# Block sums of the first MLP matrix: formed by transfers into DRAM instead of by VectorE

## The chip, the cores and the metric

The kernel runs on one core of one Trainium2 chip. The metric is device time in microseconds (us), the median over repeated executions of the same program. A profile is one further execution, taken with the hardware profiler; its times count from the first instruction.

## The reference, cut to what matters

One inference step of one layer. 576 token rows (512 of a prompt, 64 of eight short samples) are normalised and go through two parallel branches, RWKV-7 time mixing and differential attention, which sigmoid gates merge. Then comes the MLP, which the change touches:

```python
m = gate_a * (o_a @ lp['w_br_a']) + gate_b * (o_b @ lp['w_br_b'])
x = x + m @ lp['w_out']
hn = rmsnorm(x, lp['g_ffn'], NORM_EPS)
x = x + jnp.square(jax.nn.relu(hn @ lp['w_up'])) @ lp['w_down']
```

`w_up` is 1024 x 4096 and `w_down` 4096 x 1024, all in 32-bit floats.

## The kernel before, in words

Data lie transposed: channels on the 128 partitions, the 576 tokens along the free axis, mostly in two halves of 288. A 32-bit product is made from three matmuls: each weight tile is split into a rounded half `hi` (ScalarE, `act`) and a rest `lo` (VectorE, `tt`), and so are the activations.

The order of work is: the q, k and v products of the four attention heads with the attention itself between them (`qkv(h)`, `prompt`, `sample`), the RWKV pairs (`rwkv(hp)`, `chain(pr)`) with the products for `z` and the gates as filling for TensorE, the branch products (`branch_b`, then `ps_bra`), `w_out` (`ps_wo`), and the MLP (`up_pair`, `down`).

A scheduler writes the order of every engine's queue at build time. It takes instructions by priority as they become ready. `prio(at)` sets a priority; instructions outside of it have the running number of the program. Loads of weights (`load`, line 150) stand under `FEED`, ahead of all others, and wait for one of three `raw` slots; matmuls stand under `FILL`, behind all others. `tc.issue_after(ins)` ties instructions behind a given one; the loads of lines 416 to 422 and the cache pages (line 614) are tied behind the first q, k and v loads in that way. Once written, each queue runs strictly in its order on the chip. SyncE (SP) issues nearly all loads; GpSimd (POOL) issues the stores of `kTo`, `vTo`, `ob_d`, `Ss` and `Sp`, and also computes `pow` for the norms (`rpow`, lines 243 and 760).

The product with `w_up` is a Strassen-Winograd scheme on 2 x 2 blocks. For each of 16 pairs of row tiles `f1`, `f2 = f1 + 1`, the two halves along the contraction give `a11`, `a12` (of `f1`) and `a21`, `a22` (of `f2`). `up_pair` loads both rows (tile `a`, 512 KB each, line 1188), and VectorE forms four sums of blocks in tiles `s12` and `s34` (shown as `s` in the profile):

```python
tt(s12[:, 0], a21, a22, ADD)
tt(s12[:, 1], s12[:, 0], a11, SUB)
...
tt(s34[:, 0], a11, a21, SUB)
tt(s34[:, 1], a12, s12[:, 1], SUB)
```

`halve` then splits `s12`, the first row, `s34` and `a22`; seven products of 12 matmuls each follow (line 1224: `ua`, `ub`, `uc`, `ud`, `ux`), and VectorE and ScalarE combine and square the results. From the fourth pair on, four `down` products of 24 matmuls (`ps_dn`) follow each pair.

Of the kernel before, what the change touches and what calls it, by code (L numbers as in the profile page):

```python
# [8 lines left out]
F32 = mybir.dt.float32  # L9
F32R = mybir.dt.float32r  # L10
I32 = mybir.dt.int32
AF = mybir.ActivationFunctionType
# [3 lines left out]
P = 128  # L16
# [9 lines left out]
DFF = 4096  # L26
# [15 lines left out]
def tile_hybrid_step(ctx, tc, xT, xsT, ktab, vtab, s0T, ptab, w_in, vecs, w2a2, g2, lamv,  # L42
                     w_bra, w_brb, w_out, w_up, w_down, cst, bias_p, bias_s,
                     yT, kTo, vTo, Sp, Ss, sh):
    nc = tc.nc
# [9 lines left out]
    ring = {"job": 0}  # L55

    def act(out, in_, func=AF.Copy, **kw):
        ring["act"] = AE.activation(out=out, in_=in_, func=func, **kw)  # L58

    def tt(out, a, b, op, eng=None):  # L60
        ins = (eng or VE).tensor_tensor(out=out, in0=a, in1=b, op=op)  # L61
        if eng is None:
            ring["tt"] = ins

    def stt(out, a, s, b, op0, op1):
        VE.scalar_tensor_tensor(out=out, in0=a, scalar=s, in1=b, op0=op0, op1=op1)
# [16 lines left out]
    FEED, LATE, FILL = -1000000, 500000, 1000000  # L83

    @contextmanager
    def prio(at):
        was, tc.cur_priority = tc.cur_priority, at
        yield
        tc.cur_priority = was

    MUL, ADD, SUB, MAX = ALU.mult, ALU.add, ALU.subtract, ALU.max
# [20 lines left out]
    c = const.tile([P, C_END], F32, name="cst_sb")  # L112
# [103 lines left out]
    def take(n):  # L216

        while waiting and n:
            if next(waiting[0], None) is None:
                waiting.pop(0)  # L220
            else:
                n -= 1
# [40 lines left out]
    oa_d = tc.dram_tile([HB, P, NT], F32, name="oa_d")  # L263
    ob_d = tc.dram_tile([HB, P, NT], F32, name="ob_d")
    gt_d = tc.dram_tile([2 * KT, P, NT], F32, name="gt_d")

    zp = pool("zp", stack=ph1)
    zw = pool("zw", 2, stack=ph1)
# [353 lines left out]
    def sample(b):  # L622
        kps = early.pop(b, None) or pages(b, True)
        if b + 1 < NB:
            early[b + 1] = pages(b + 1, True)
        vps = pages(b, False)
        pss = cbank(b % 2, f"psb{b}")
        quads = [(h, slice(32 * h, 32 * h + 32)) for h in range(HB)]

        for h, o in quads:  # L630
            mm(pss[o, P:2 * P], qbd[:, b, h], kps[1][:, h])
        with tc.issue_after(ring["mm"].ins):
            for h, o in quads:
                mm(pss[o, 0:P], qbd[:, b, h], kps[0][:, h])
            for h, o in quads:
                mm(pss[o, 256:320], qbd[:, b, h], kT[:, h, NPR:])
        sc = scs[b % 2]
        stt(sc[:, :256], pss[:, :256], 0.125, bs[:, :256], MUL, ADD)
        stt(sc[:, 256:320], pss[:, 256:320], 0.125, bs[:, 256 + 64 * b:320 + 64 * b], MUL, ADD)
        nmx = stat.tile([P, 1], F32, tag="nms", name=f"nms{b}")  # L640
        VE.tensor_reduce(out=nmx, in_=sc[:, :320], axis=AX.X, op=MAX, negate=True)
        z = stat.tile([P, 1], F32, tag="zs", name=f"zs{b}")
        act(sc[:, :320], sc[:, :320], AF.Exp, bias=nmx, accum_out=z)
        rz = stat.tile([P, 1], F32, tag="rzs", name=f"rzs{b}")
        VE.reciprocal(out=rz, in_=z)
        tt(rz, rz, cw, MUL)
        yield 1
        pt = bank(f"pts{b}")
        for j in range(3):
            tr(pt[:, j * P:(j + 1) * P], sc[:, j * P:(j + 1) * P], ident)  # L650
        pT = ap.tile([P, 3, P], F32, tag="pT", name=f"pT{b}", bufs=2)
        act(pT, pt[:, :384].rearrange("p (j r) -> p j r", j=3))
        yield 1
        po = bank(f"pos{b}")
        for j in range(3):
            for h, o in quads:
                mm(po[o, :P], pT[:, j, o], vps[j][:, h] if j < 2 else vtok[:, 4, h],
                   start=(j == 0), stop=(j == 2))
        orw = ap.tile([P, P], F32, tag="orw", name=f"orw{b}", bufs=2)
        act(orw, po[:, :P], scale=rz)  # L660
        yield 1
        pq = bank(f"pq{b}")
        mm(pq[:, :32], orw, c[:, C_SEL:C_SEL + 32])
        act(osT[:, b], pq[:, :32].rearrange("p (h q) -> p h q", h=HB))
    for h in range(HB):
        if h:
            qkv(h)
        for cc in range(2):
            GE.tensor_copy(
                out=qbd[64 * cc:64 * cc + 64, :, h, 8 * cc:8 * cc + 8],  # L670
                in_=qT[64 * cc:64 * cc + 64, h, NPR:].rearrange("p (b q) -> p b q", b=NB))
        ot = ap.tile([P, 4, P], F32, tag="ot", name=f"ot{h}", bufs=2)
        ss = stat.tile([P, 4], F32, tag="ss", name=f"ss{h}")
        qk = stacks(h)
        if h < HB - 1:
            for qb in range(4):
                feed(prompt(h, qb, ot, ss, *qk))
    waiting += [shifted(12), shifted(13)] + zs(0)
    for n in range(4):
        for unit in (prompt(HB - 1, n, ot, ss, *qk), sample(2 * n), sample(2 * n + 1)):  # L680
            feed(unit)
            fill(18)
# [366 lines left out]
    def run(*stages):  # L1049
        for hp in stages:  # L1050
            while Pt[8 + hp] is None:
                take(2)
            next(gens[hp], None)
# [2 lines left out]
    ga = [gate(g) for g in range(KT)]  # L1056
    waiting += ga[:5]
    run(0, 0)
    take(221)
    run(0, 1, 1)  # L1060
    take(106)
    run(1)
    chain(0)
    run(2, 0, 1)
    take(190)
    run(2, 3)
# [61 lines left out]
    for i, d in enumerate((0, 4, 1, 5, 2, 6, 3, 7)):  # L1128
        xr = wt_.tile([P, NT], F32, tag="xr", name=f"xr{d}")
        with prio(FEED + 1000 * (ring["job"] + 1) - 1):  # L1130
            nc.sync.dma_start(out=xr, in_=xT[:, d])
        hf = hfs[d] = wt_.tile([P, NT], F32, tag="hf", name=f"hf{d}", bufs=3)
        k = d % 4

        def ev(ps, t0, n, d=d, k=k, xr=xr, hf=hf):
            x, h = ya[:, d, t0:t0 + n], hf[:, t0:t0 + n]
            tt(x, ps, xr[:, t0:t0 + n], ADD)
            act(h, x, scale=v(V_GF + d))
            if d < 4:
                if t0 == 0:  # L1140
                    put("b11", k, h)
                else:
                    t1 = wt_.tile([P, 288], F32, tag="t", name=f"t1_{k}", bufs=4)
                    tt(t1, h, hf[:, :288], SUB)
                    hfs["t1", k] = t1
                    put("t1", k, t1)
            elif t0:
                for n, x, y in (("t2", h, hfs["t1", k]), ("t3", h, hfs[k][:, 288:])):
                    t = hfs[n] = wt_.tile([P, 288], F32, tag="t", name=f"{n}_{k}", bufs=4)
                    tt(t, x, y, SUB)  # L1150
                    put(n, k, t)
                put("b22", k, h)
            else:
                put("b21", k, h)
                t4 = wt_.tile([P, 288], F32, tag="t", name=f"t4_{k}", bufs=4)
                tt(t4, h, hfs["t2"], SUB)
                put("t4", k, t4)
        dense(w_out[d], KT, mh, ml, HALF[::1 if d < 4 else -1], ev, f"wo{d}")

        for j, (t0, n) in enumerate(HALF):  # L1160
            o = acc[:, t0:t0 + n]
            if i == 0:
                act(o, ya[:, d, t0:t0 + n], AF.Square)
            else:
                sq = cbank(j, f"sq{d}{j}")[:, :n]
                act(sq, ya[:, d, t0:t0 + n], AF.Square)
                tt(o, o, sq, ADD)
# [12 lines left out]
    def up_pair(f1):  # L1180
# [2 lines left out]
        for f in (f1, f2):  # L1183
            qs[f] = hq_pool.tile([P, 2, NT], F32R, tag="q", name=f"q{f}")
        with prio(FEED + 1000 * (ring["job"] + 1)):
            rows = [sp_.tile([P, 2, 4, P], F32, tag="raw", name=f"a{f}", bufs=3) for f in (f1, f2)]
            for r, f in zip(rows, (f1, f2)):
                nc.sync.dma_start(out=r.rearrange("p i k w -> p (i k) w"), in_=w_up[f])
        (a11, a12), (a21, a22) = ([r[:, i] for i in range(2)] for r in rows)
        s12, s34 = (sp_.tile([P, 2, 4, P], F32, tag="s", name=f"s{i}_{f1}", bufs=2) for i in (12, 34))  # L1190

        def halve(x, two, after):

# [6 lines left out]
                tt(lo, x, f32(hi), SUB)  # L1200
            return [(hi[:, i], lo[:, i]) for i in range(2)] if two else (hi, lo)

        with prio(FEED + 1000 * (ring["job"] + 1) + 90):
            tt(s12[:, 0], a21, a22, ADD)
            tt(s12[:, 1], s12[:, 0], a11, SUB)
        S1, S2 = halve(s12, True, 1)
        A11, A12 = halve(rows[0], True, 2)
        with prio(FEED + 1000 * (ring["job"] + 3) + 90):
            tt(s34[:, 0], a11, a21, SUB)
            tt(s34[:, 1], a12, s12[:, 1], SUB)  # L1210
        S3, S4 = halve(s34, True, 5)
        A22 = halve(a22, False, 7)

# [16 lines left out]
        def out(f, half, c, r=None):  # L1230

            sp = slice(288 * half, 288 * half + 288)
            r = c if r is None else r
            act(r, c, AF.Relu)
            act(r, r, AF.Square)
            act(qs[f][:, 0, sp], r)
            tt(qs[f][:, 1, sp], r, f32(qs[f][:, 0, sp]), SUB)
# [267 lines left out]
```

## Time and profile before

| what | value |
|---|---|
| median of 3 runs | 999.91 us (999.71 to 1001.37) |
| span of the profiled execution | 1004.0 us, 24422 instructions |
| TensorE matmul busy | 975.5 us (97%) |
| VectorE busy | 689.5 us (69%) |
| ScalarE busy | 497.3 us (50%) |
| GpSimd busy | 88.3 us (9%) |
| DMA | 105.75 MB, mean 105 GB/s |

The profiled execution has no time of its own beside its span, which runs from the first to the last instruction; that span is 4.1 us above the median. In the rows of the profile, PE is TensorE, PEld its weight loads, DVE is VectorE, ACT ScalarE, POOL GpSimd, SPq and POOLq the instruction queues of SyncE and GpSimd. The last two figures before a bar are the busy time of a group and the mean of one instruction in ns.

### The profile page before, as it was taken

The page shows a single profiled execution, that of the slowest core. Times are in us where ns is not written, and L with a number is a line of the kernel's source. Part 1 is how long each engine was busy: PE and PEld are TensorE (multiplying, and loading weights), DVE is VectorE, ACT ScalarE, POOL GpSimd, SP SyncE. Part 2 cuts the span into 40 slices and gives each one's busy share as a digit, 9 for nine tenths or more (in the row PEclk, how much of TensorE's full clock was granted, in tenths as well). Part 3 has the DMA queues.
Part 4 walks back from the last instruction along what each step waited for, and adds up shares of the span by engine and source line. Part 5 has one row for each costly group of instructions (what it writes and reads, how often), then busy time and mean ns, then how long its engine had stood idle before and what let it go on. Part 6 is the DMA issues. An engine that isn't in the chain of part 4 may idle for free.

```text
span 1004.0 us, 24422 instructions
## 1 busy us (share of the span) xinstructions
PE 975.5 (97%) x10012; PEld 919.9 (92%) x10012; DVE 689.5 (69%) x1459; ACT 497.3 (50%) x1094; POOL 88.3 (9%) x171
## 2 busy tenths in 40 slices
PE   8999999899999999999999999999999999999996
PEld 8999998898887878888889999999999999999996
DVE  6698666774946669445588798966666666666744
ACT  6576555354435344443344666644444444444732
POOL 2511001301010340000300000000000000000001
PEclk9999999999989989999999999999999999999998
DMA  7312673121111225222377642222222222221402
GB/s 265 142 66 88 204 221 120 54 64 45 43 47 57 69 87 171 80 70 102 106 215 237 195 152 74 95 85 95 85 85 95 84 85 85 85 84 44 128 10 95
DMA packets 50833, 105.75 MB, mean 105 GB/s; under 512 B 6066, under 2 KB 8114, under 8 KB 50594
## 3 DMA queue, kind: packets, MB, share of 16 engines
q1 hardware_dynamic: 47442, 96.95, 30.2%
q0 software_dynamic: 1648, 5.35, 1.4%
q8 instruction: 79, 1.29, 0.5%
q10 hardware_dynamic: 1632, 1.89, 0.5%
q14 instruction: 32, 0.26, 0.1%
HBM read 89.38 MB, written 14.78 MB: 104 GB/s over the span
## 4 chain that ended last, share of the span: by engine, by line
PE 86%; DVE 6%; ACT 3%; DMA 2%; issue 2%; POOL 1%; SPq 0%; DVEq 0%; POOLq 0%; ACTq 0%
PE ps_dn L72 21%; PE ps_g L72 9%; PE ps_z L72 8%; PE ua L1224 5%; PE ux L1224 5%; PE ps_wo L72 4%; PE uc L1224 3%; PE ud L1224 3%; PE ub L1224 3%; PE ps_k L72 2%; PE ps_brb L72 2%; PE pch L72 2%; PE ps_q L72 2%; PE ps_v L72 2%; PE pA L72 2%
## 5 line engine op out<-in xcount | busy, mean ns | idle before, releaser
L72 PE MATMUL ps_dn<-q,hi_dn 128*128 128x288 f32 x768 | 154.7, 296 | 0.0
L72 PEld LDWEIGHTS ps_dn<-q,hi_dn 128*128 128x128 f32 x768 | 122.8, 188 | 1.5
L72 PE MATMUL ps_dn<-q,lo_dn 128*128 128x288 f32 x384 | 113.2, 295 | 0.0
L72 PE MATMUL ps_g<-xl,hi_g 128*128 128x288 f32 x256 | 80.2, 313 | 0.0
L72 PE MATMUL ps_g<-xh,lo_g 128*128 128x288 f32 x256 | 79.3, 310 | 0.0
L72 PE MATMUL ps_g<-xh,hi_g 128*128 128x288 f32 x256 | 79.2, 310 | 0.0
L72 PEld LDWEIGHTS ps_dn<-q,lo_dn 128*128 128x128 f32 x384 | 72.1, 188 | 0.0
L72 PE MATMUL ps_z<-xh,lo_z 128*128 128x288 f32 (+1 forms) x224 | 69.6, 311 | 0.0
L72 PE MATMUL ps_z<-xh,hi_z 128*128 128x288 f32 (+1 forms) x224 | 68.3, 305 | 0.0
L72 PE MATMUL ps_z<-xl,hi_z 128*128 128x288 f32 (+1 forms) x224 | 67.6, 302 | 0.0
L61 DVE TENSOR_TENSOR ya<-ya,ps_dn 128x288 f32<-128x288 f32 x96 | 43.4, 453 | 29.3 <-PE ps_dn L72 29.3
L58 ACT ACTIVATE hi_dn<-raw_dn 128x512 fp32r<-128x512 f32 x48 | 30.1, 628 | 57.0 <-PE ps_dn L72 57.0
L1224 PE MATMUL ua<-h_b,hi 128*128 128x288 f32 x256 | 53.2, 298 | 0.0
L1224 PE MATMUL ux<-h_t,hi 128*128 128x288 f32 x256 | 52.3, 296 | 0.0
L58 ACT ACTIVATE c<-c 128x288 f32<-128x288 f32 x112 | 48.4, 439 | 7.5 <-DVE c L61 5.8
L72 PEld LDWEIGHTS ps_g<-xh,hi_g 128*128 128x128 f32 x256 | 49.0, 191 | 2.9 <-issue 1.6
L72 PEld LDWEIGHTS ps_g<-xl,hi_g 128*128 128x128 f32 x256 | 49.0, 191 | 1.9
L72 PEld LDWEIGHTS ps_g<-xh,lo_g 128*128 128x128 f32 x256 | 49.1, 192 | 1.4
L58 ACT ACTIVATE hi<-a 128x1024 fp32r<-128x1024 f32 (+1 forms) x32 | 27.1, 846 | 42.0 <-PE ps_dn L72 34.3
L72 PE MATMUL ps_dn<-q,w 128*128 128x320 f32 (+1 forms) x336 | 46.4, 298 | 0.0
L61 DVE TENSOR_TENSOR lo<-s,hi 128x1024 fp32r<-128x1024 f32 x32 | 39.2, 1225 | 10.2 <-ACT hi L58 10.0
L72 PEld LDWEIGHTS ps_dn<-q,w 128*128 128x128 f32 x336 | 45.3, 190 | 0.1
(395 smaller groups left out, 2801.7 us busy)
## 6 DMA issues: line engine op xcount, KB each, us to landing
a<-in_w_up_dram SPq DMA_DIRECT2D x32, 512.0 KB, 3.3
raw_dn<-in_w_down_dram SPq DMA_DIRECT2D x64, 256.0 KB, 2.9
raw_g<-in_w_in_dram SPq DMA_DIRECT2D x32, 256.0 KB, 3.2
raw_z<-in_w_in_dram SPq DMA_DIRECT2D x28, 256.0 KB, 3.0
gt_d<-gg SPq DMA_DIRECT2D x16, 288.0 KB, 2.5
g<-gt_d SPq DMA_DIRECT2D x16, 288.0 KB, 3.7
kp<-in_ktab_dram SPq DMA_DIRECT2D x16, 256.0 KB, 4.0
vp<-in_vtab_dram SPq DMA_DIRECT2D x16, 256.0 KB, 3.7
```

Of the source, the lines that this page charges most:

```text
L58: ring["act"] = AE.activation(out=out, in_=in_, func=func, **kw)
L61: ins = (eng or VE).tensor_tensor(out=out, in0=a, in1=b, op=op)
L72: ring["mm"] = PE.matmul(out=out, lhsT=lhsT, rhs=rhs, start=start, stop=stop)
L1224: ring["mm"] = PE.matmul(out=ps[:, :288], lhsT=l[:, k], rhs=hb[blk][:, h, k], start=start and i == 0, stop=i == 11, skip_group_check=skip)
```

## The change

The four sums are no longer made by VectorE. A scratch `us_d` of 16 x 128 x 4 x 512 floats (16 MB) in DRAM takes their place. The generator `block_sums(4)` fills it in four parts of 4 MB: for each part four copies from `w_up` into the slots 0 to 3 (1 MB each, from SP), and later four accumulating transfers (1 MB each, from POOL) that add `a22` to slot 0, `a21` to slot 2, slot 0 to slot 1 and slot 1 to slot 3. Each call of `next` writes one tick into the program: three before the heads 1 to 3, two among the samples, one before `take(221)` and one after `chain(0)`. In the seven ticks, part `t` is copied in tick `t`; its first two additions are written in tick `t + 1`, the others in `t + 2` and `t + 3`. No priority and no `issue_after` stands around them. As transfers only add, the second row of each pair enters with its sign turned; the tiles `t1` to `t4` and a scale of -1 before the Relu of `f2` turn it back.

`up_pair` now loads `s12`, row `f1` (`a1`), `s34` (512 KB each) and `a22` alone (256 KB). The first three share five `raw` slots of 4 KB per partition (before: three for `a`, two for `s`); `a22` takes one of the three `raw` slots of the ring that the `w_down` loads also use.

```diff
+    us_d = tc.dram_tile([DFF // 256, P, 4, 4 * P], F32, name="us_d")
+
+    def block_sums(n):
+
+        blk = w_up.rearrange("(g o) p (i k) w -> o i p g (k w)", o=2, i=2)
+        dst = us_d.rearrange("g p s c -> s p g c")
+        a11, a12, a21, a22 = (blk[o, i] for o in range(2) for i in range(2))
+        for t in range(16 // n + 3):
+            part = lambda a, t: a[:, n * t:n * t + n]
+            for s, src in ((0, a21), (2, a11), (1, a11), (3, a12)):
+                if t < 16 // n:
+                    nc.sync.dma_start(out=part(dst[s], t), in_=part(src, t))
+            for s, src, late in ((0, a22, 1), (2, a21, 1), (1, dst[0], 2), (3, dst[1], 3)):
+                if 0 <= t - late < 16 // n:
+                    nc.gpsimd.dma_start(out=part(dst[s], t - late), in_=part(src, t - late), accum_op=ADD)
+            yield
...
+    sums_ = block_sums(4)
     for h in range(HB):
         if h:
+            next(sums_)
             qkv(h)
...
     for n in range(4):
+        if n % 2:
+            next(sums_)
         for unit in (prompt(HB - 1, n, ot, ss, *qk), sample(2 * n), sample(2 * n + 1)):
...
     run(0, 0)
+    next(sums_)
     take(221)
...
     chain(0)
+    next(sums_)
     run(2, 0, 1)
...
-                    tt(t1, h, hf[:, :288], SUB)
+                    tt(t1, hf[:, :288], h, SUB)
...
+                    if n == "t2":
+                        stt(t, h, -1.0, hfs["t1", k], MUL, SUB)
+                    else:
+                        tt(t, h, hfs[k][:, 288:], SUB)
...
-                tt(t4, h, hfs["t2"], SUB)
+                stt(t4, hfs["t2"], -1.0, h, MUL, SUB)
...
-            rows = [sp_.tile([P, 2, 4, P], F32, tag="raw", name=f"a{f}", bufs=3) for f in (f1, f2)]
-            for r, f in zip(rows, (f1, f2)):
-                nc.sync.dma_start(out=r.rearrange("p i k w -> p (i k) w"), in_=w_up[f])
-        (a11, a12), (a21, a22) = ([r[:, i] for i in range(2)] for r in rows)
-        s12, s34 = (sp_.tile([P, 2, 4, P], F32, tag="s", name=f"s{i}_{f1}", bufs=2) for i in (12, 34))
+            s12, a1, s34 = (sp_.tile([P, 2, 4, P], F32, tag="raw", name=f"{n}{f1}", bufs=5)
+                            for n in ("s12", "a1", "s34"))
+            a22 = ring["pool"].tile([P, 4, P], F32, tag="raw", name=f"a22{f1}", bufs=3)
+            flat = lambda t: t.rearrange("p i k w -> p (i k w)")
+            nc.sync.dma_start(out=flat(s12), in_=us_d[f1 // 2, :, 0:2].rearrange("p s c -> p (s c)"))
+            nc.sync.dma_start(out=a1.rearrange("p i k w -> p (i k) w"), in_=w_up[f1])
+            nc.sync.dma_start(out=flat(s34), in_=us_d[f1 // 2, :, 2:4].rearrange("p s c -> p (s c)"))
+            nc.sync.dma_start(out=a22, in_=w_up[f2][:, 4:8])
...
-        with prio(FEED + 1000 * (ring["job"] + 1) + 90):
-            tt(s12[:, 0], a21, a22, ADD)
-            tt(s12[:, 1], s12[:, 0], a11, SUB)
         S1, S2 = halve(s12, True, 1)
-        A11, A12 = halve(rows[0], True, 2)
-        with prio(FEED + 1000 * (ring["job"] + 3) + 90):
-            tt(s34[:, 0], a11, a21, SUB)
-            tt(s34[:, 1], a12, s12[:, 1], SUB)
+        A11, A12 = halve(a1, True, 2)
...
-            act(r, c, AF.Relu)
+            act(r, c, AF.Relu, scale=-1.0 if f == f2 else 1.0)
```

More of the change, by code (lines that the diff above doesn't have):

```diff
@@ L1147, in ev @@
             elif t0:
-                for n, x, y in (("t2", h, hfs["t1", k]), ("t3", h, hfs[k][:, 288:])):
+                for n in ("t2", "t3"):
                     t = hfs[n] = wt_.tile([P, 288], F32, tag="t", name=f"{n}_{k}", bufs=4)
-                    tt(t, x, y, SUB)
+                    if n == "t2":
+                        stt(t, h, -1.0, hfs["t1", k], MUL, SUB)
+                    else:
+                        tt(t, h, hfs[k][:, 288:], SUB)
                     put(n, k, t)
```

## The prediction, made before the changed kernel ran

> **What bounds the kernel now.** I read the page first (busy shares, slices, DMA queues), then the stretches around the MLP, then the chain of waits, and last the order of the queues at the start.
>
> ```profile
> PE 975.5 (97%) x10012; PEld 919.9 (92%) x10012; DVE 689.5 (69%) x1459; ACT 497.3 (50%) x1094; POOL 88.3 (9%) x171
> DMA  7312673121111225222377642222222222221402
> q1 hardware_dynamic: 47442, 96.95, 30.2%
> PE 86%; DVE 6%; ACT 3%; DMA 2%; issue 2%; POOL 1%; SPq 0%; DVEq 0%; POOLq 0%; ACTq 0%
> ```
>
> TensorE is busy 97% of the span and is 86% of the chain that ends last; VectorE is 6% of it. The stretches (us, then busy time of PE, PEld, DVE, ACT, POOL, clock, DMA share, GB/s) say where TensorE still has idle time:
>
> ```profile
> 500.00:524.00 24.00, 22.58 (x145) 18.96 (x144) 18.79 (x36) 10.26 (x26) 3.97 (x4) 1.00 0.66 206
> 524.00:552.00 28.00, 26.60 (x196) 25.79 (x195) 22.90 (x55) 11.25 (x24) 0.00 (x0) 1.00 0.73 236
> 552.00:568.00 16.00, 15.21 (x111) 14.52 (x110) 10.68 (x24) 8.70 (x20) 0.00 (x0) 1.00 0.62 205
> 604.00:640.00 36.00, 36.00 (x267) 35.06 (x267) 31.62 (x60) 23.85 (x56) 0.00 (x0) 1.00 0.23 74
> 760.00:920.00 160.00, 160.00 (x1197) 159.07 (x1196) 108.64 (x196) 74.69 (x139) 0.00 (x0) 1.00 0.26 86
> ```
>
> From 604 us on, where the sums are used, TensorE never stops: 36.00 of 36 and 160.00 of 160. VectorE is at 88% in the first (31.62 / 36) and 68% in the second (108.64 / 160), off the path in both. The idle time ahead of the MLP is 1.42 + 1.40 + 0.79 = 3.6 us (500 to 568).
>
> **The change part by part.** *Removed: the sums.*
>
> ```profile
> L61 DVE TENSOR_TENSOR s<-a 128x512 f32<-128x512 f32 x16 | 11.0, 688 | 0.3 <-DMA a<-in_w_up_dram 0.3
> L61 DVE TENSOR_TENSOR s<-s,a 128x512 f32<-128x512 f32 x16 | 10.9, 684 | 0.0
> L61 DVE TENSOR_TENSOR s<-a,s 128x512 f32<-128x512 f32 x16 | 10.9, 684 | 0.0
> L61 DVE TENSOR_TENSOR s<-a,a 128x512 f32<-128x512 f32 x16 | 10.9, 683 | 0.0
> 555.58 7.19 DMA a<-in_w_up_dram
> 563.85 0.64 DVE s L61 x2
> ```
>
> 64 instructions, 11.0 + 3 x 10.9 = 43.7 us of VectorE. The last two rows are the chain of waits. The sums touch it at one place only, the first pair, where VectorE stands at the head of its queue for the first `a` (7.19 us) and then makes sums (0.64 us). What TensorE loses there is at most the 0.79 us of the stretch 552 to 568, so the sums are worth 0 to 0.8 us; I take -0.4. The other 15 pairs are worth nothing, since TensorE is their cover. The turned signs cost nothing: the same number of operations on the same shapes.
>
> *Added in the MLP.* Per pair 1.75 MB instead of 1 MB, four issues on SP instead of two. The DMA share there is 0.23 to 0.26; three quarters more of half the traffic leaves it under 0.4, so 15 pairs hide it. For the first pair and what is prefetched behind it, five slots of 512 KB and one of 256 KB are loaded where three of 512 KB were: 1.25 MB, 3.9 us of all engines by the 3.1 us per MB below, in a stretch at 0.62. That costs 0 to 3.9; I take 1, as ScalarE now waits for `s12` where VectorE waited for `a`. The first `s12` itself waits for the sums only if these are later than 555 us. `a22` takes one of three slots from the `w_down` loads.
>
> ```profile
> ACT hi_dn L58 <- PE ps_dn L72: 57.0, 23, 2.6
> ACT w L58 <- DMA raw_dn<-in_w_down_dram: 5.3, 8, 1.2
> raw_dn<-in_w_down_dram SPq DMA_DIRECT2D x64, 256.0 KB, 2.9
> ```
>
> The halving of `w_down` waits for matmuls to free a slot (57.0 us) and hardly for data (5.3); the rows are from the list of waits and the DMA issues. With five loads per pair in three slots, a load is still some two products (2 x 3.2 us: 24 matmuls of 12.89 / 96 each, by the chain below) ahead of its use, against 2.9 us to land: 0. Were that lead gone, each of 48 products could lose up to 2.9 us, 139 us in all, which is the upper end of this term and unlikely.
>
> ```profile
> 785.78 12.89 PE ps_dn L72 x96
> 809.87 12.89 PE ps_dn L72 x96
> ```
>
> *Added ahead of the MLP: the copies.* 16 copies of 1.05 MB (4 x 128 rows of 2 KB) on SP's queue. Queue 1 moved 96.95 MB in 30.2% of the 1004 us of its 16 engines: 0.302 x 1004 / 96.95 = 3.13 us per MB, so 3.3 us per copy if a byte that is read and written costs what a loaded one does (lower end), 6.6 us if reading and writing are charged apart (upper end). Nothing in the trace copies DRAM to DRAM; loads and stores are equally near, so I take the middle, 4.9 us, which makes 16 x 4.9 = 78 us. [...]
>
> Over the 440 us from the heads to the MLP the engines are four fifths idle, so volume is no trouble. What decides is *where in SP's queue the copies come*. They need no data and no slot, and they carry neither a priority nor a tie. What the scheduler does with such instructions, the timeline of POOL shows beside a row of the chain:
>
> ```profile
> 14.31 0.10 POOL L426 MEMSET Z<- 128x1 f32 x1 [2.59 <-DVE lo_k L61]
> 14.92 0.10 POOL L426 MEMSET Z<- 128x1 f32 x1 [0.50 <-DVE lo_v L61]
> 125.71 0.11 POOL L426 MEMSET Z<- 128x1 f32 x1 [6.01 <-DVE P L66]
> 112.78 2.27 PE ps_z L72 x17
> ```
>
> The first `Z` clearings stand in the program behind all four heads (`shifted(12)`, `shifted(13)`); their products start at 112.78 us. They run at 14.31 and 14.92, as soon as their slots are free, some 100 us ahead; the third waits for a slot until 125.71. So the place of a call of `next` sets only the rank among ready instructions. SP's queue at that time, then ScalarE's timeline, the waits of SP's queue and two rows of the DMA issues (size, us to landing):
>
> ```profile
> 10.80 1.01 SPq L150 DMA_DIRECT2D raw_q<-in_w_in_dram  x2
> 12.78 0.57 SPq L420 DMA_DIRECT2D wl<-in_w2a_dram  x1
> 14.18 0.43 SPq L422 DMA_DIRECT2D wg<-in_g_dram  x1
> 19.74 0.33 SPq L150 DMA_DIRECT2D raw_k<-in_w_in_dram  x1
> 34.33 0.33 SPq L150 DMA_DIRECT2D raw_q<-in_w_in_dram  x1
> 32.95 0.62 ACT L58 ACTIVATE hi_k<-raw_k 128x512 fp32r<-128x512 f32 x1
> 44.67 0.63 ACT L58 ACTIVATE hi_q<-raw_q 128x512 fp32r<-128x512 f32 x1 [0.34 <-ACT sc L58]
> SPq L291 <- DMA vec<-in_vecs_dram: 0.7, 1, 0.7
> bs<-in_bias_s_dram SPq DMA_DIRECT2D x1, 384.0 KB, 7.5
> raw_k<-in_w_in_dram SPq DMA_DIRECT2D x8, 256.0 KB, 3.3
> ```
>
> `wg` ends at 14.6; from there to 19.74 SP only waits for a slot, and later loads wait again until 34.33. Into the first gap the scheduler can put all copies of all four ticks, or at least some ten (0.43 to 0.57 us per issue), the rest into the second. Weight loads behind them wait twice over. Transfers of one queue share its engines in turn (`bs`, 384 KB, issued right behind the 1 MB of `bp`, takes 7.5 us, where 256 KB take 3.3), and SP stops at a limit of outstanding transfers (an `x` load, which needs nothing, waits for the transfer of `vec`).
>
> The lead of the loads is small. The second half of `raw_k` of head 1 is issued at 19.74, lands at 23.0 and is needed at 32.95: 9.9 us. `raw_q` of head 2 is issued at 34.33 and needed at 44.67. With all 16 copies ahead of it, it lands at 14.6 + 16 x 4.9 + 3.3 = 96.3, which is 51.6 us late; with 3.3 us per copy 26 us, with 6.6 us 79 us. What is late next is TensorE's `ps_q` of head 2, and nothing covers it: its queue is in order and nearly full there. Later loads come at their old distance. So the copies cost 51.6 us.
>
> *The additions.* 16 of 1.05 MB on POOL's queue, a kind that the trace does not show. Bounds: 3.3 us each, if the sum is free, to 9.9 us, if both reads and the write are charged: 53 to 158 us of engine time, mostly behind the copies. Their issue, and two `pow` steps of POOL's queue:
>
> ```profile
> L711 POOL DMA_DIRECT2D ob_d<-obs x1 | 0.8, 797 | 1.3 <-DVE nr L69 1.3
> 28.32 1.17 POOL L243 TENSOR_TENSOR r<-r,mhalf 128x5 f32<-128x5 f32 x1 [12.15 <-DVE m L1291]
> 63.99 1.04 POOL L243 TENSOR_TENSOR rr<-rr,mhalf 128x4 f32<-128x4 f32 x1 [7.72 <-DVE rr L69]
> ```
>
> 512 rows took 0.80 us to issue (`obs`), so 16 take 13 us of an engine that is 9% busy: 0. Beside weight loads they can at worst double the 3.3 us of a load, still inside the lead of 9.9: 0. [...] What they hold up is POOL: an addition waits for its copies, and behind it in the queue stand `r` (28.32, the norm that every evacuation of head 0 needs) and `rr` (63.99). The first copies land about 14.6 + 4 x 4.9 + 2 = 36, later than `r`, so I put `r` ahead and take 0; if the scheduler's order has additions ahead of `r`, the cost is below.
>
> *The sum:* -0.4 + 1 + 0 + 51.6 + 0 = +52 us. The span of the profile (1004.0) is 4.1 us above the median of 999.91; the differences apply to either, so 999.9 + 52 = 1052. I give 1050.
>
> **The rivals.**
>
> *Hidden.* If transfers to one scratch are ordered one behind the other, or if the ticks do spread them, at most two copies stand ahead of a load: 2 x 4.9 = 9.8 us against a lead of 9.9. Then all is hidden and the time is 1000, within 2. For it: the DMA share of 0.1 to 0.3 over the heads and RWKV. Against: the `Z` rows.
>
> *Partly hidden.* The copies come in four bursts of 4, one per tick. Each exposes up to 4 x 4.9 - 9.9 = 9.7 us, less what a later slot gives back: 5 to 40 us, 1005 to 1040.
>
> *POOL becomes the wait.* Additions stand ahead of `r`, and `r` comes after the last copies, at 14.6 + 78 = 93 instead of 28.3: +65, and if chained additions stand ahead of it too, two more waits of 5 to 12 us each and more: 1065 to 1100.
>
> *Faster.* VectorE's relief lets the branch products and `w_out` run closer: the 3.6 us of idle time between 500 and 568 is all there is, and it has to give over 2 us with the copies wholly hidden. Two thirds of it and a luckier order in the RWKV part: 997.5. It decides from the point where no weight load is over 9.9 us late.
>
> **How the numbers follow.** Copies ahead of the loads: 0.46 (own range 1026 to 1080). POOL: 0.11. Partly hidden: 0.16. Hidden: 0.14. Faster: 0.13. Under 0.2%, or 2 us, a measurement of this kernel can tell nothing from no change; the three runs differ by 1.7 us. So faster 0.13, same 0.14, slower 0.73. The range is 998 to 1085: it leaves out most of "faster" and the upper half of POOL's, 0.18 together.
>
> **What would show it.** In the changed profile: SP's issues of the copies (`us_d` from `w_up`) between 14 and 35 us; `raw_k`, `raw_v` and `raw_q` loads with tens of us to landing there; `hi_q` of head 2 near 95 us instead of 44.67; the slices of PE under 9 in the third to fifth fortieth and DMA at 7 or more; from 600 us on, shifted, the same 809.87 - 785.78 = 24.1 us per pair with VectorE some 2.7 us per pair less busy. The prediction is wrong if the copies lie apart over 100 us or more, if they run well under 3.3 us each, or if `w_down` halvings wait for data in the MLP.

## The result, and the profile after

The changed kernel takes 1076.1 us (1075.66 to 1079.16) against 1000.0 us (999.71 to 1001.37) of the kernel before on the same chip: 1.0768 times as long, interval 1.075 to 1.0787. The forecast was 1050 us, with a range of 998 to 1085. The profiled execution has a span of 1077.3 us, 73.3 more than that of before. One execution of a kernel below, that with plain copies, took 1177.88 us at a granted clock of 0.745 (0.976 and more in the others) and does not enter its ratio.

From the page of the changed kernel: busy shares, the slices of TensorE and of the DMA engines, the two queues, and the chain:

```profile
PE 982.9 (91%) x10012; PEld 927.2 (86%) x10012; DVE 654.9 (61%) x1395; ACT 497.6 (46%) x1094; POOL 107.0 (10%) x187
PE   8970864898999999999999999999999999999996
DMA  8999999742111111342225875343334343332312
q1 hardware_dynamic: 60498, 126.31, 36.0%
q0 software_dynamic: 10096, 22.13, 10.0%
PE 74%; DMA 9%; DVE 6%; issue 6%; ACT 3%; POOL 2%; SPq 0%; DVEq 0%; POOLq 0%; ACTq 0%
```

VectorE lost its 64 instructions (1459 to 1395), and TensorE, with the same 10012 matmuls, is no longer busy 97% of the span but 91%. The loss is at one place: the third to eighth of the 40 slices of PE read 7, 0, 8, 6, 4 and 8 where DMA stands at 9 from the second to the seventh. In the chain of waits that ended last, DMA rises from 2% to 9% of the span. Stretches of the changed kernel (columns as in the prediction):

```profile
60.00:80.00 20.00, 14.61 (x97) 14.33 (x98) 11.49 (x29) 8.83 (x28) 4.36 (x4) 0.83 1.08 302
80.00:100.00 20.00, 0.79 (x6) 0.55 (x5) 0.00 (x0) 0.00 (x0) 1.26 (x1) 0.57 1.09 270
20.00:200.00 180.00, 113.26 (x788) 107.28 (x787) 77.83 (x189) 62.16 (x166) 43.78 (x74) 0.80 1.01 261
833.00:993.00 160.00, 160.00 (x1198) 159.09 (x1197) 93.47 (x168) 74.76 (x140) 0.00 (x0) 1.00 0.37 116
```

The same 180 us of the kernel before hold 174.73 us of matmuls at a DMA share of 0.41:

```profile
20.00:200.00 180.00, 174.73 (x1558) 163.66 (x1557) 130.45 (x320) 97.72 (x252) 38.25 (x84) 0.99 0.41 130
178.43 2.18 POOL L760 TENSOR_TENSOR nr<-nr,mhalf 128x10 f32<-128x10 f32 x1
```

The second row is the first norm of the RWKV part in POOL's timeline. After the change it stands at 254.84, 76.4 us later; the whole loss of 73.3 us is made ahead of it. In the MLP's 160 us TensorE is saturated as before, while VectorE went from 108.64 to 93.47: nothing waited for it. POOL's timeline of the changed kernel, then two rows of its chain, then waits:

```profile
88.10 1.26 POOL L280 DMA_DIRECT2D us_d<-us_d  x1 [17.61 <-DMA us_d<-in_w_up_dram]
105.23 1.24 POOL L280 DMA_DIRECT2D us_d<-us_d  x1 [15.87 <-DMA us_d<-us_d]
106.00 1.55 POOL L243 TENSOR_TENSOR rr<-rr,mhalf 128x4 f32<-128x4 f32 x1
254.84 2.17 POOL L780 TENSOR_TENSOR nr<-nr,mhalf 128x10 f32<-128x10 f32 x1
```

```profile
88.10 16.84 DMA us_d<-us_d
106.46 1.09 POOL rr L243
```

```profile
POOL us_d L280 <- DMA us_d<-in_w_up_dram: 61.1, 6, 18.8
POOL us_d L280 <- DMA us_d<-us_d: 56.0, 4, 16.3
DVE ot L69 <- POOL rr L243: 48.3, 4, 30.7
```

`rr` of head 0 ran at 63.99 before; now it stands behind eight additions of POOL's queue, six of which wait there for another transfer to the scratch, the last two for 17.61 and 15.87 us; the chain runs through the last addition but one and `rr`. So three explanations were open: SP (the copies' place in SP's queue, the prediction's), POOL (its in-order queue), and volume (the engine time of all the transfers).

### The profile page after: what moved, and what is told of

Read it like the earlier page. It is cut to its first block, busy times and chain, and to the rows that moved or that the text cites. A ratio compares the mean times of both kernels' runs of the same rounds, so it can differ in the third digit from the quotient of the medians.

```text
span 1077.3 us, 24511 instructions
## 1 busy us (share of the span) xinstructions
PE 982.9 (91%) x10012; PEld 927.2 (86%) x10012; DVE 654.9 (61%) x1395; ACT 497.6 (46%) x1094; POOL 107.0 (10%) x187
## 3 DMA queue, kind: packets, MB, share of 16 engines
q0 software_dynamic: 10096, 22.13, 10.0%
## 4 chain that ended last, share of the span: by engine, by line
PE 74%; DMA 9%; DVE 6%; issue 6%; ACT 3%; POOL 2%; SPq 0%; DVEq 0%; POOLq 0%; ACTq 0%
PE ps_dn L72 19%; PE ps_g L72 9%; PE ps_z L72 7%; PE ua L1246 5%; PE ux L1246 4%; DMA us_d<-in_w_up_dram 4%; PE ps_wo L72 3%; PE uc L1246 2%; PE ub L1246 2%; PE ud L1246 2%; PE ps_brb L72 2%; PE pch L72 2%; PE ps_k L72 2%; DMA us_d<-us_d 2%; PE pA L72 2%
```

## The experiments

A ratio is to the runs of the kernel before in the same comparison (medians 1001.4 to 1002.4 us). Additional engine time is the share of queues 1 and 0 times the span, less the same of the run that has only the MLP's side.

**The copies without the additions.** The additions (the three lines that end in `accum_op=ADD`) are left out, so the scratch holds unsummed blocks; the copies stay where they are.

> The 16 additions are left out (the sums in the scratch are incomplete); the 16 copies stand at the same places of SP's queue as in the changed kernel. Theory POOL (the additions hold GpSimd's queue while they wait, and the pow steps and stores behind them come late): without additions nearly all of the +76 is gone, 1000 to 1008 us, and rr of head 0 runs near 64 us as before. Theory SP (the prediction's step: copies stand ahead of weight loads): the copies are unchanged, so at least 40 of the 76 us stay, 1040 to 1076 us, with hi_q of head 2 tens of us later than its 44.67. Theory volume (the 16 engines are full, whoever asks): half to two thirds of the bytes stay, 1020 to 1040.

Measured: 1001.91 us, ratio 0.9998 (0.9982 to 1.0015). Two stretches, the queues, and a row of SP's timeline of this run:

```profile
40.00:60.00 20.00, 19.50 (x137) 17.78 (x135) 18.49 (x48) 13.46 (x39) 6.49 (x23) 1.00 1.01 344
60.00:80.00 20.00, 19.69 (x142) 18.64 (x142) 18.14 (x45) 13.62 (x37) 3.29 (x5) 1.00 0.98 334
```

```profile
q1 hardware_dynamic: 60498, 126.31, 39.1%
q0 software_dynamic: 1648, 5.35, 1.4%
```

```profile
56.34 4.09 SPq L277 DMA_DIRECT2D us_d<-in_w_up_dram  x4
```

The engines are full (1.01, 0.98), the copies stand between the weight loads in SP's queue, and TensorE loses nothing. The prediction's main step falls: of the three forecasts only POOL's (1000 to 1008) holds. As the additions take both their waits on POOL and their engine time with them, this run does not tell these two apart.

**The MLP's side alone.** No transfers to the scratch; `up_pair` loads tiles of the same sizes from `w_up`, other blocks than the sums.

> No copies and no additions; the MLP loads tiles of the same sizes from w_up where the sums would be (the MLP's products use the second row in place of the sums). All theories that put the loss ahead of the MLP: within 0.2% of before, 998 to 1002 us; the prediction's own terms for this side were -0.4 and +1 us. If a22 in the ring of w_down or the larger loads cost anything, it shows here as over 1002.

Measured: 1002.36 us, ratio 0.9999 (0.9985 to 1.0013): within 1.4 us either way, the missing sums and the additional 0.75 MB per pair are together worth nothing (the kernel before takes 1002.42 us in the same comparison).

```profile
q1 hardware_dynamic: 52050, 109.53, 33.8%
q0 software_dynamic: 1648, 5.35, 1.5%
```

These rows give the base of the engine time: 35.3% of 998.8 = 352.6 us, and with the rows above 3.3 us per copy: (0.391 x 999.3 - 0.338 x 998.8) / 16.

**The front alone.** The kernel before with the generator and its seven ticks; the MLP does not read the scratch.

> The kernel before, with the 16 copies and 16 additions put where the change puts them; the MLP is that of before and does not read the scratch. If the whole loss is made ahead of the RWKV part, as the stretches of the changed kernel say (its first RWKV norm comes 76.4 us late, its end 73.3 us), this takes 1073 to 1079 us. If the MLP's four loads per pair have any share, it lies below: 1060 to 1070.

Measured: 1076.76 us, ratio 1.076 (1.0737 to 1.0783). That is inside the forecast of 1073 to 1079: the transfers to the scratch make the whole loss.

**POOL freed.** Copies and additions in the same order, but what stands behind the additions leaves POOL's queue (a reciprocal stands in for the power of -0.5):

```diff
-        nc.gpsimd.dma_start(out=kTo[:, h], in_=kT[:, h])
-        nc.gpsimd.dma_start(out=vTo[h], in_=vT)
+        nc.scalar.dma_start(out=kTo[:, h], in_=kT[:, h])
+        nc.scalar.dma_start(out=vTo[h], in_=vT)
...
-        rpow(rr, ss, 1.0 / P, 1e-5)
+        ts(rr, ss, 1.0 / P, MUL, 1e-5, ADD)
+        VE.reciprocal(out=rr, in_=rr)
...
-        nc.gpsimd.dma_start(out=ob_d[h, :, :NPR], in_=obh)
+        nc.scalar.dma_start(out=ob_d[h, :, :NPR], in_=obh)
...
-            GE.tensor_copy(
+            VE.tensor_copy(
```

> Copies and additions stay in the same order on both queues, but what stands behind additions on GpSimd in the attention is moved away: stores of kTo, vTo and ob_d to ScalarE's queue, the qbd copies and rr to VectorE (rr as a reciprocal, so the scaling of the attention's output differs). Theory POOL: most of the loss is gone, 1005 to 1030, though the additions run as early and the engines are as full. Theory volume or SP: 1055 to 1080, since neither the bytes nor the loads' places change.

Measured: 1054.62 us, ratio 1.0522 (1.0497 to 1.0547). That is at the lower edge of what was forecast for volume or SP and far above POOL's range. 52 of the 76 us stay though no wait for `rr` is left in this run; some 24 go with POOL's queue. This is a difference and not a share: where POOL no longer holds up the attention, ScalarE waits for late loads (below), and what the moved work costs on its new queues was not measured by itself. A stretch of this run, a wait, and two rows of SP's timeline:

```profile
20.00:200.00 180.00, 132.96 (x1079) 125.31 (x1082) 94.46 (x241) 74.52 (x201) 33.06 (x55) 0.87 1.07 286
```

```profile
ACT hi_q L58 <- DMA raw_q<-in_w_in_dram: 27.9, 3, 26.3
```

```profile
63.13 14.03 SPq L277 DMA_DIRECT2D us_d<-in_w_up_dram  x4
77.26 12.37 SPq L150 DMA_DIRECT2D raw_q<-in_w_in_dram  x2
```

With additions beside them four copies take 14.03 us to issue (4.09 without), and ScalarE waits up to 26.3 us for the `raw_q` loads behind them. So the prediction's picture, loads held up behind copies in SP's queue, does occur, but only with additions on top of the copies: in the run without them the engines were full too, from 40 to 60 us (1.01).

**Half of the additions; plain copies in their place.** The first run keeps the eight additions from the weights (`((0, a22, 1), (2, a21, 1))`), the second has all 16 without `accum_op=ADD`.

> All 16 copies and only the 8 additions that take both operands from the weights; the two sums that need a second step are left unfinished. The engines get 16 x 3.0 + 8 x 5.8 = 94 us of work instead of 142. If the loss is the time for which the engines are full beyond what the copies alone can take for nothing, it goes down more than in proportion: 1005 to 1030 us. If it is a price per addition, half: 1036 to 1042. If it is the chained additions' waits on POOL, nearly all goes: 1000 to 1005.

> The 16 additions become plain copies of the same bytes from the same places of POOL's queue; the sums are therefore not formed. Theory kind (an accumulating transfer keeps the 16 engines busy for 5.8 us, a copy for 3.0): the engines have 32 x 3.0 = 96 us of work instead of 142, POOL's waits shrink with it, 1010 to 1035 us. Theory volume (33.6 MB more in this stretch are too many, whatever the kind): 1060 to 1076. Theory POOL (what costs is that POOL's queue stands for predecessors, ten times in a row): each wait is one transfer's landing, so it stays within a third of what it was, 1050 to 1076.

Measured: 1035.26 us, ratio 1.0336 (1.0305 to 1.0368), and 1037.91 us, ratio 1.0364 (1.0343 to 1.0385). Half of the additions cost a little less than half: that is 5 us outside the first forecast of the first text and 0.7 us under its second, a price per addition. Plain copies missed the kind theory's range by 3 us and the other two by 12 and more. Queues of the first, then of the second:

```profile
q1 hardware_dynamic: 60498, 126.31, 37.3%
q0 software_dynamic: 5872, 13.74, 5.9%
```

```profile
q1 hardware_dynamic: 60498, 126.31, 37.5%
q0 software_dynamic: 6000, 22.13, 6.0%
```

Queue 0 gives 5.8 us of all engines per addition ((0.059 x 1034.0 - 0.015 x 998.8) / 8; from the changed kernel's 10.0%, 5.8 too) and 2.9 us per plain transfer ((0.060 x 1035.9 - 15.0) / 16). Set beside the loss:

| kernel | additional engine time, us | loss, us |
|---|---|---|
| copies only | 52 | -0.5 |
| copies, 8 additions | 94 | 33.8 |
| copies, 16 plain on POOL | 98 | 36.5 |
| changed kernel | 143 | 76.1 |

The two middle runs differ twofold in the number of transfers on POOL and in kind, yet with the same engine time they lose the same. The loss goes with engine time on top of the copies: these had already filled the engines from 40 to 80 us, and each further us goes with some 0.8 us of loss (33.8 / 42, 36.5 / 46, 76.1 / 91). An addition takes twice the time of a plain transfer and costs twice as much. That engine time alone sets the price is not shown, though. The two runs wait for different things, eight additions (first two rows) mostly for weight loads, plain copies (last row) for POOL's `rr`:

```profile
ACT hi_q L58 <- DMA raw_q<-in_w_in_dram: 12.2, 2, 11.8
DVE ot L69 <- POOL rr L243: 8.3, 3, 5.9
```

```profile
DVE ot L69 <- POOL rr L243: 31.6, 4, 20.2
```

So POOL's queue has a part in the 0.8, and that the two losses are equal may be in part chance.

**Additions moved into the RWKV part.** Eight go behind `nb` of pair 1 and eight behind `var` of pair 1, on POOL, where the DMA share is low:

```diff
+        with tc.issue_after(after.ins):
+            for s in kinds:
+                for t in range(4):
+                    g = slice(4 * t, 4 * t + 4)
+                    nc.gpsimd.dma_start(out=dst[s][:, g], in_=srcs[s][:, g], accum_op=ADD)
```

> The copies as in the changed kernel; the additions are tied behind GpSimd instructions of the RWKV part ahead of two stretches in which its queue has nothing urgent: 8 behind nb of pair 1 (about 281 us before), 8 behind var of pair 1 (about 375 us). All is computed. Theory POOL: the loss is gone but for what the copies cost alone, that is the time of the run without additions plus 0 to 8 us. Theory SP: as the changed kernel, 1060 to 1076. Theory volume: as the run without additions plus little, 1020 to 1045.

Measured: 1023.9 us, ratio 1.0223 (1.02 to 1.0245). That is in volume's range and 14 us above POOL's; nearly 55 of the 76 us come back. A stretch with the second burst of this run:

```profile
380.00:400.00 20.00, 14.35 (x168) 13.26 (x166) 15.03 (x28) 5.79 (x11) 5.48 (x5) 0.95 1.10 231
```

**Additions one by one, with two controls.** Each addition behind one of the 16 gate stores, 8 to 23 us apart:

```diff
-        nc.sync.dma_start(out=gt_d[g], in_=gg)
+        with tc.issue_after(nc.gpsimd.dma_start(out=gt_d[g], in_=gg).ins):
+            next(adds)
```

> Copies where the change puts them. The 16 additions one at a time, each on POOL behind the store of one of the 16 gate products (moved from SP's to POOL's queue), some 13 us apart from 288 to 505 us; everything is computed. Theory: one addition alone takes the engines 5.8 us and is gone before the next, a load beside it comes at most about 6 us later, inside the lead of some 10 us: 999 to 1006 us. Rival (any addition makes the loads beside it late, wherever it is, as 16 in two bursts cost 22 us): 1015 to 1030. Second rival (POOL's queue, waiting for each gate product, holds up the RWKV work behind it): also 1010 or more, with POOL's stores named in the waits of the other engines.

Measured: 1033.28 us, ratio 1.0344 (1.0291 to 1.0397): a clear miss, worse than two bursts and 3 us above the first rival's range. The controls have the same stores with plain copies, and the stores alone:

> The additions spread one by one behind the gate stores (1033 us), each replaced by a plain copy of the same bytes at the same place; the sums are not formed. Theory kind: a plain copy holds the engines half as long, loads and instruction fetches beside it are hardly late, 1000 to 1010 us, and TensorE's stops of 2 us with no releaser in the dense stretch 440 to 460 are gone. Rival (it is POOL's queue, or any transfer of 1 MB): 1025 to 1035.

> The control for the spread additions: the 16 gate stores stand on POOL as there, with no additions; the sums are not formed. If the move of the stores had no part in the 31 us, this takes 999 to 1004 us. If POOL's waiting for the gate products holds up the RWKV work, it takes 1010 to 1030, and the additions are to that extent innocent there.

Measured: 1020.43 us, ratio 1.0196 (1.0141 to 1.025), and 1008.62 us, ratio 1.0059 (1.0038 to 1.008). The moved stores cost 6.5 us themselves, which was between the two forecasts. Over them, plain copies cost 11.8 us (some 6 either way) and additions 25, again about twofold; both ranges of the first of the two texts were missed. The engines are full in one place only here: between 280 and 540 us the DMA share of the run with additions is 0.46 to 0.83, but for 1.04 from 380 to 400. Where these transfers strike is seen in the waits of the run with additions, then of that with plain copies, then of the stores alone:

```profile
PE pZ L72 <- issue: 9.2, 6, 2.5
ACT obh L58 <- DMA ob<-ob_d: 8.3, 4, 5.6
```

```profile
PE pZ L72 <- issue: 5.3, 4, 2.5
```

```profile
PE pZ L72 <- issue: 3.0, 3, 1.1
```

`issue` means that TensorE waited for nothing that the profile shows; plain copies make it less but not gone, where the kind theory had it gone (the kernel before has 1.8 us of it). The loads of `ob` also come later: 8.3 us of waits against 5.0 with plain copies and 2.5 with the stores alone. In the timeline of the run with additions all such stops of TensorE between 440 and 460 us stand here; below, the rows of the instruction queue in the windows 441.3:441.4, 446.8:446.9 and 457.4:457.5 (packets, MB, share of 16 engines' 0.1 us):

```profile
443.61 1.03 PE L72 MATMUL pW<-X,DM 32*32 32x32 f32 x64 [1.92 <-issue]
449.13 0.34 PE L72 MATMUL pZ<-W,Y 32*32 32x32 f32 x18 [1.40 <-issue]
453.53 0.52 PE L72 MATMUL pZ<-W,Y 32*32 32x32 f32 x36 [0.21 <-issue]
459.83 0.67 PE L72 MATMUL pZ<-W,Y 32*32 32x32 f32 x55 [2.12 <-issue]
```

```profile
q8 instruction: 1, 0.02, 59.1%
q8 instruction: 1, 0.02, 58.7%
q8 instruction: 1, 0.02, 60.9%
```

Each packet takes 0.1 x 16 x 0.59 = 0.94 us, ends at 442.3, 447.8 and 458.4, and TensorE goes on 1.3 to 1.4 us after its end, all three times. The only other packet of these 20 us (window 451.3:451.4) ends at 452.3, and the fourth stop, of 0.21 us, is over 1.2 us later; large matmuls had run until then. So here TensorE most likely stands for its own instructions: in this stretch it runs hundreds of 32 x 32 matmuls. No run tested that by itself. The Trainium skill ("Runtime: NRT & Kernel Launch", section "Instruction fetch mechanics") says that an engine's next page of instructions comes by a DMA queue of its own in blocks of 16 KiB and that the cost is mostly hidden; the packets (0.02 MB) agree. If this is the cause, the hiding fails beside additions by 1.4 to 2.1 us in three of these four places.

**Additions into the MLP.** Four behind gate stores at 300 to 349 us, where the spread ones cost TensorE nothing (20.00 and 20.00 of 20 from 320 to 360), the other 12 behind a one-column copy of `c22` on POOL, two in each of the first two pairs and one in each of the next eight.

> Copies where the change puts them. The four additions of the first four pairs go behind four gate stores on POOL (303 to 353 us, where the spread additions cost TensorE nothing); the other 12 go into the MLP, each on POOL behind a one-column copy of that pair's third sum: two in each of the first two pairs, one in each of the next eight. Everything is computed. Theory: an addition costs time only where the engines are full, or where TensorE runs hundreds of small matmuls and must fetch instructions; neither holds in the MLP, where TensorE runs large products and the DMA share is 0.37: 999 to 1006 us. Rival (an addition makes every load beside it late by several us wherever it is, and w_down's loads have a lead of only some 6 us): 12 additions x 1 to 3 us, 1012 to 1040, with the w_down halvings waiting for data.

Measured: 1010.72 us, ratio 1.009 (1.0073 to 1.0107). Stretches and two waits of this run:

```profile
640.00:680.00 40.00, 33.94 (x240) 33.70 (x239) 18.70 (x36) 13.60 (x26) 4.05 (x5) 0.91 0.89 227
720.00:760.00 40.00, 40.00 (x301) 39.74 (x300) 21.22 (x41) 15.67 (x30) 1.43 (x2) 1.00 0.67 171
```

```profile
ACT hi_dn L58 <- DMA raw_dn<-in_w_down_dram: 37.0, 7, 15.0
SPq L1230 <- DMA us_d<-us_d: 10.7, 1, 10.7
```

The time lies between the two forecasts. One addition per pair costs nothing (40.00 of 40). Where two stand in a row, the second building on the first, SP stood 10.7 us before a load of the sum itself, with `w_down` loads behind it: 6.06 us of TensorE. Whether their company did it or the sum's coming late for its load, this run does not tell, and the next changes both.

**Never two together.** Two early ones at 183 and 208 us, five behind gate stores, nine in the MLP, one per pair.

> As the kernel with 12 additions in the MLP (1010.7 us), but no two additions close together: one behind the copy of nb at 181 us, one behind a Z clearing at 206, five behind gate stores at 303 to 363, nine in the MLP, one per pair, each ahead of the pair that needs it by more than a pair. There two additions in a row made SP wait 10.7 us for the second with w_down loads queued behind (halvings waited 15.0 us, TensorE lost 6.06 us from 640 to 680). Theory: that was all of its loss but some 3 us from the moved gate stores: 1000 to 1006 us, with 40.00 of 40 busy in every stretch of the MLP. Rival (any addition beside TensorE's work costs): 1008 to 1015. Since the MLP by itself gains nothing from the sums being ready (1002.4 against 1002.4), neither theory expects a time under that of the kernel before by more than 0.2%.

Measured: 1004.26 us, ratio 1.003 (1.0018 to 1.0041), as forecast. The stretch that lost 6.06 us, in this run:

```profile
640.00:680.00 40.00, 39.75 (x298) 39.39 (x298) 21.09 (x40) 15.30 (x30) 1.79 (x3) 1.00 0.77 206
```

So all but 2.6 of the 76 us (1.8 to 4.1 by the interval) were the additions' place, time and company. What remains is 0.3% above the kernel before, and no experiment points to a version that beats it, since the sums were worth nothing to begin with.

## Why the prediction was right or wrong

*Right: direction, range, and the MLP's side.* Slower was forecast at 0.73 and came, inside the range, but by another mechanism than the one forecast; that is luck. The terms of -0.4, +1 and 0 (sums, loads, `w_down` ring) are confirmed only as a sum near 0: 1002.36 against 1002.42 us, 1.4 either way.

*Wrong: the step that carried the sum, "so the copies cost 51.6 us".* Alone they cost -0.5. Three parts of it failed. The place: they were not bunched between 14 and 35 us. Rows of SP's timeline of the changed kernel show them between the weight loads, from 20.86 to 139 us, over 100 us apart, which the prediction itself had named as a sign that it is wrong:

```profile
20.86 0.64 SPq L277 DMA_DIRECT2D us_d<-in_w_up_dram  x1
64.86 13.79 SPq L277 DMA_DIRECT2D us_d<-in_w_up_dram  x4
128.97 10.06 SPq L277 DMA_DIRECT2D us_d<-in_w_up_dram  x2
```

The `Z` clearings, from which the bunching was read, stood on an idle queue; on SP's, the loads rank ahead as soon as they have a slot, and the copies fill what is left. The price: 3.3 us each, the lower end, where I took 4.9. The wait: with the copies alone the loads of `raw_q`, `raw_k` and `raw_v` landed within 8.7 us of their issue (within 6.1 before), inside the lead of 9.9, and ScalarE waited for them 0.5 us in all. One reading behind this step was wrong too: an `x` load's wait for `vec` shows no limit of SP's queue, as `vec` is issued from ScalarE's. That SP does stand where the engines are full is shown by the four copies that took 14.03 us to issue with POOL freed and 4.09 with the copies alone.

*Wrong: "beside weight loads they can at worst double the 3.3 us of a load ... 0" for the additions.* This is the term that was mis-sized: 0 forecast, about 76 measured. Their price lay inside the bounds (5.8 us, between 3.3 and 9.9), but the sum of engine time was never set against the stretch where they run. 53 + 93 us were added to 74 us in use; 220 us do not go into 180. Nor is going into it enough: the plain copies' 98 + 74 = 172 us cost 36.5 us, with the DMA share at 0.96 to 1.02 in every 20 us from 20 to 140. The prediction set the transfers against 440 us of engines "four fifths idle", while the order on POOL and SP put nearly all between 21 and 190 us; and before the change the DMA share was 0.41 there and 0.34 from 100 to 540 us, so two thirds idle at most. The other part of the term is POOL's own queue, put at 0 because `r` would stay ahead: `rr` was the one that came late. The Trainium skill ("DMA: Bandwidth & Descriptors", section "Queues, rings and completion order") says that a DMA engine serves its queue rows by turns, packet by packet. That may hold, and no run here tests it, but it says nothing of volume: with POOL freed, ScalarE waited up to 26.3 us for a `raw_q` load. An addition is also not a copy in price: the Trainium skill ("Collectives: The Full Stack", section "Stop ④ — SDMA + CCE: where bytes move and the add happens") counts an adding transfer of a collective as read, read and write with the add free in between. Here 5.8 us stand against 2.9 us for the plain transfer at the same places, which agrees if the second read is what is paid; no run separates it from the add.

*The rivals.* "POOL becomes the wait" (0.11) named a real part, with another victim: one addition did come ahead of `r`, but `r` still ran at 29.23 us (28.32 before), and `rr` stood behind eight additions until 106.00. POOL's queue makes some 24 of the 76 us. "Hidden" is what happens to the copies alone. "Partly hidden" put its cost on the copies, and "Faster" on VectorE's relief; neither is worth anything by the runs. That 1050 lay only 26 us off is owed to two errors against each other, copies priced at 52 instead of 0 and additions at 0 instead of 76.

*Open:* how the loss of the changed kernel divides between late loads and POOL's queue, beyond the 52 and 24 us of the run with POOL freed; how much of the 25 us of the spread additions is instruction fetching (6.2 us more of `pZ` waits are seen) and how much late loads (5.8 us more of waits for `ob`); and why 16 in two bursts (21.5 us) cost no more than 16 apart.

## What to carry to other kernels

Before calling a background transfer free, add its engine time to what is in use in the very stretch where the queues will put it, and compare with the length of that stretch; the mean share of the span hid it here. Price an accumulating transfer at twice a copy, as it measured here, let a chain of two land well ahead of the load that needs it, and put nothing behind them on an in-order queue that the critical path needs. Ask first whether the work taken away was on the path: 43.7 us of VectorE under a saturated TensorE were worth 0.

## What the hardware showed that was not expected

A DRAM-to-DRAM copy of 1.05 MB costs the 16 engines 2.9 to 3.3 us, as much as loading its bytes (3.13 us per MB), although it reads and writes DRAM; one that adds costs 5.8 us in the crowd and 6.7 us when spread ((0.129 x 1032.3 - 25.2) / 16, the stores alone being 25.2). An adding transfer also takes 528 packets ((10096 - 1648) / 16) where the plain one takes 272 ((6000 - 1648) / 16), for the same 22.13 MB on queue 0. Copies filled the engines (1.01 and 0.98) for 40 us without harm to in-order loads between them. Beside additions TensorE stopped for up to 2.1 us with no releaser, in the four places shown until 1.2 to 1.4 us after a packet of the instruction queue. In the 20 us in which TensorE was busy for 0.79 us its granted clock was 0.57 (80 to 100 us).
